# One decoder step on one core: the gate moved into the GpSimd scaling, the samples' keys loaded ahead of the cache copies, three sample products issued later

## The chip, the core and the metric

The kernel runs on one core of a Trainium2 chip. A core has five engines with instruction queues of their own: TensorE (PE, matrix products; PEld is its weight load), VectorE (DVE), ScalarE (ACT), GpSimd (POOL) and SyncE (SP), which here only issues DMAs. Each engine takes its instructions in the order in which they stand, and a waiting instruction holds up all that stand behind it on that engine. The metric is the time of one execution on the device in microseconds (us), as the median of the runs; lower is better.

## The reference

One layer of a hybrid decoder runs over a prompt of 1024 rows and over 8 samples of one row each. A projection feeds three groups of heads; what the change touches are the attention group ("NSA", 8 query heads, 2 KV heads of 64), and the samples' part of the recurrent group.

```python
def masked_softmax(s, mask):
    ...
    p = jnp.exp(s - m)
    return p / jnp.maximum(jnp.sum(p, axis=-1, keepdims=True), 1e-30)

def gate_mix(g, o_c, o_s, o_w):            # g = sigmoid of 24 projected columns, 3 per head
    return g[..., 0:1] * o_c + g[..., 1:2] * o_s + g[..., 2:3] * o_w
```

`o_c` attends to compressed blocks, `o_s` to the selected blocks (for this prompt length all the causal rows), and `o_w` to a window of 512 rows. A sample's window is `win_buf` (511 rows of its cache and one new row), and the shifted window is an output too:

```python
    kw = jnp.concatenate([win_buf, rows_w_new], axis=0)
    o_w = window_attend(q, qpos, kw[:, 0], kw[:, 1], kpos)
    return gate_mix(gates, o_c, o_s, o_w), kw[s_len:]
```

The recurrent group (RWKV-7) takes one step of its state for each sample, normalizes the result by head, and multiplies it into the sample's row.

## The kernel before

**Stages.** Phase 1 (`phase1`, up to about 515 us) projects the prompt and runs its recurrence. It also makes the gates: `do_g` turns the 24 gate columns, takes a sigmoid by way of tanh, and replaces it by its reciprocal (line 426), so that `self.gates` holds 1/gate.

Phase 2 (`phase2`, about 515 to 844 us) is the prompt's attention, with the samples' work woven in. The prompt is cut into 8 tiles of 128 rows, taken from tile 7 down to tile 0, and each tile into 4 units of two heads. For a unit, `attn_scores` does the following for each of the two branches b (0: causal, 1: window):

- PE makes the scores `p_s` in PSUM.
- DVE adds the mask, takes the row's minimum of the negated scores (`nm`) and writes `p` (line 1322; in the profile a custom instruction and a short read of the accumulator).
- ACT takes the exponential in place and sums the rows into `sm` (line 1323).
- DVE makes `fac` = 1 / (max(sm, 1e-30) / gate) in two instructions (lines 1345 and 1346).
- POOL multiplies `p` by `fac` (line 1349, one instruction for each of two heads, over 128 partitions and up to 1024 elements).

Then PE turns `p` (`p_pT<-ident,p`, `attn_turn`) by way of PSUM, ACT and DVE copy the turned blocks to `pt` in alternation (lines 1293 and 1295), and PE multiplies them with the values (`p_o<-pt,vs`, `attn_out`). DVE multiplies the result into `cat`. The compressed branch (`attn_cmp`, once a tile) makes a factor `c_r` for 8 heads in the same way (lines 1267 and 1269) and multiplies its `pcq` on DVE.

**What sets the order.** `InOrder` keeps PE's instructions in the order in which the program is written, and adds up an estimate of their time (`clock`). Four generators run beside the units: queries, tiles, samples and the samples' rests. After each piece of a unit `slot` lets those continue whose announced time has passed: a `yield 9.0` says "not before 9 us of PE's estimated time". So these numbers decide where in PE's order a sample's product stands. On the other engines the scheduler decides, by priority. DMAs stand in the order of SP's queue.

**The samples.** `sample_setup` normalizes and rotates the samples' queries and keys: a first product `p_sn` (sums of squares), later `p_sh` (the halves swapped), later `p_ts` (turned to rows). `sample_mem` and then `sample_win` each take two groups of four samples. In `sample_win`, `load` issues for each sample a copy of its cache from DRAM to DRAM (line 1800, 511 KB), the keys (`wkt`, line 1801, 256 KB), a DVE copy that puts the new key in column 0 (line 1802; it waits for the keys to land), the values (`wxv`, line 1805) and the new value's row (line 1806, which waits until the values have landed). Then PE makes `p_wS` from four samples' keys. `four_keys` takes the buffers for the keys: for each group two of a kind of their own, and two from a ring of three that `sample_mem` also uses. The load of a tile's queries (`q<-q_d`, line 1220) is in the same SP queue, and waits until POOL has split the queries (`qhl`, line 1226) that last stood in that buffer.

`sample_rwkv` takes the recurrent step on DVE, sends the result through DRAM once to bring it into rows (`rw_a<-sy_d`), normalizes it in some 20 DVE instructions (lines 2163 to 2174), and PE turns the result (`p_sy`). Then `nsa_ahead` loads `w1a` into the buffer that `p_sy` has read, and the first pages of the samples' cache.

Phase 3 (844 us to the end) makes the output projection and the samples' compressed and selected attention.

Of the kernel before, what the change touches and what calls it, by code (L numbers as in the profile page):

```python
# [15 lines left out]
OP = mybir.AluOpType  # L16
# [32 lines left out]
def bc(ap, shape):  # L49
    return ap.to_broadcast(shape)  # L50


def wait(us):
    yield us
# [60 lines left out]
class Step:  # L115
# [302 lines left out]
    def do_g(self, H, pieces, j):  # L418
        turned = self.to_tok(H, pieces, 24, 10)

        def gates():
            nc, ps = self.nc, turned()
            g = self.gates[:, H * 4:H * 4 + 4, :]
            nc.scalar.activation(g, ps[:, :, :24], AF.Tanh, scale=0.5)
            nc.vector.tensor_scalar(g, g, 0.5, 0.5, op0=OP.mult, op1=OP.add)
            nc.vector.reciprocal(g, g)
        return gates

    def phase1(self):
# [809 lines left out]
    def attn_cmp(self, i):  # L1239

        nc = self.nc
        V, A, G, PE = nc.vector, nc.scalar, nc.gpsimd, self.te
        qs = self.qs[i]
        gate = self.gates[:, i, :].rearrange("p (h b) -> p h b", b=3)
        p2 = self.pM.tile([128, 4, 2, 64], F32, name="p_sc", tag="m")
        x = 56 - 8 * i
        PE.matmul(p2[:].rearrange("p a b c -> p (a b) c"), self.cmask[:, 120:248],
                  bc(self.cmask[:, None, x:x + 64], [128, 8, 64]), start=True, stop=False)
        for j in range(4):
            for g in range(2):  # L1250
                for n, ck in enumerate((self.ckh, self.ckl)):
                    PE.matmul(p2[:, j, g], qs[:, 4 * g + j, :], ck[:, 0, g * 64:g * 64 + 64], start=False, stop=(j == 3 and g == 1 and n == 1))
            if j == 1:
                yield 0.1
        pcq = self.we.tile([128, 8, 64], F32, name="pcq", tag="pcq")
        v3 = lambda x: x.rearrange("p a b c -> p (a b) c")
        st = self.small.tile([128, 8], F32, name="c_m")
        V.tensor_reduce(st[:], v3(p2[:]), axis=AX.X, op=OP.max)
        V.tensor_scalar(st[:], st[:], -1.0e20, None, op0=OP.max)
        V.tensor_tensor(pcq[:], v3(p2[:]), bc(st[:, :, None], [128, 8, 64]), op=OP.subtract)  # L1260
        yield
        A.activation(pcq[:], pcq[:], AF.Exp)
        sm = self.small.tile([128, 8], F32, name="c_s")
        V.tensor_reduce(sm[:], pcq[:], axis=AX.X, op=OP.add)
        rc = self.small.tile([128, 8], F32, name="c_r")
        gh = lambda x: x.rearrange("p (h g) -> p g h", g=2)
        V.scalar_tensor_tensor(gh(rc[:]), gh(sm[:]), 1e-30, gate[:, :, 0].rearrange("p (g h) -> p g h", g=2),
                               op0=OP.max, op1=OP.mult)
        V.reciprocal(rc[:], rc[:])
        V.tensor_tensor(pcq[:], pcq[:], bc(rc[:, :, None], [128, 8, 64]), op=OP.mult)  # L1270
        yield 6.0 if i < 7 else 4.0
        self.pcT[i] = self.pt_copy(lambda j: pcq[:, 2 * j:2 * j + 2, :].rearrange("p a b -> p (a b)"), "c")
        yield
# [24 lines left out]
    def attn_scores(self, i, g, hp, Ps):  # L1298

        nc = self.nc  # L1300
        V, A, PE = nc.vector, nc.scalar, self.te
        n1 = 128 * (i + 1)
        w0 = max(0, 128 * (i - 4))
        split = i >= 4
        qs = self.qs[i]
        gate = self.gates[:, i, :].rearrange("p (h b) -> p h b", b=3)
        nm = self.small.tile([128, 2, 2], F32, name="nm")
        sm = self.small.tile([128, 2, 2], F32, name="sm")

        def scores(ps, q, b, c0, c1):  # L1310
            u, o, w = c0 // 512, c0 % 512, c1 - c0
            PE.matmul(ps, q, self.kh[u][:, 2 * b + g, o:o + w], start=True, stop=False)
            PE.matmul(ps, q, self.kl[u][:, 2 * b + g, o:o + w], start=False, stop=True)

        def weigh(ps, h, b, c0):
            x, w = Ps[h, b][:, :n1 - c0], n1 - c0
            if b == 1 and split:
                m = bass.AP(tensor=self.bmask.tensor, offset=self.bmask.offset, ap=[self.bmask.ap[0], [832, 2], [1, 320]])
                halves = lambda t: t.rearrange("p (a c) -> p a c", a=2)
            else:  # L1320
                m, halves = self.bmask[:, 1152 - w:1152], lambda t: t
            V.tensor_tensor_reduce(halves(x), halves(ps), m, -1.0, 3.0e38, op0=OP.add, op1=OP.min, accum_out=nm[:, h, b:b + 1])  # L1322
            A.activation(x, x, AF.Exp, scale=-1.0, bias=nm[:, h, b:b + 1], accum_out=sm[:, h, b:b + 1])  # L1323

        f = self.small.tile([128, 2, 2], F32, name="fac")
        hd = 4 * g + 2 * hp
        for b in range(2):
            c0 = w0 if b else 0
            for h in range(2):
                Ps[h, b] = self.pp.tile([128, 1024 if b == 0 else 640], F32, name="p", tag=f"p{b}")  # L1330
            if split:
                for h in range(2):
                    ps = self.pS.tile([128, 1024], F32, name="p_s", tag="s")
                    scores(ps[:, c0:512], qs[:, hd + h, :], b, c0, 512)
                    scores(ps[:, 512:n1], qs[:, hd + h, :], b, 512, n1)
                    weigh(ps[:, c0:n1], h, b, c0)
                    if h == 0:
                        yield
            else:
                ps = self.pS.tile([128, 2, 512], F32, name="p_s", tag="s")  # L1340
                for h in range(2):
                    scores(ps[:, h, :n1], qs[:, hd + h, :], b, 0, n1)
                for h in range(2):
                    weigh(ps[:, h, :n1], h, b, 0)
            V.scalar_tensor_tensor(f[:, :, b], sm[:, :, b], 1e-30, gate[:, hd:hd + 2, 1 + b], op0=OP.max, op1=OP.mult)
            V.reciprocal(f[:, :, b], f[:, :, b])  # L1346
            for h in range(2):
                x = Ps[h, b][:, :n1 - c0]
                nc.gpsimd.tensor_scalar(x, x, f[:, h, b:b + 1], None, op0=OP.mult)  # L1349
            yield  # L1350

    def attn_turn(self, i, Ps, n, m):
# [259 lines left out]
    def sample_setup(self):  # L1612

        tc, nc, I, O = self.tc, self.nc, self.I, self.O
        V, A, G, PE = nc.vector, nc.scalar, nc.gpsimd, self.te
# [14 lines left out]
        x, sq, xr = (self.we.tile([128, 8, NS], F32, name=f"s_x{k}") for k in range(3))  # L1630
# [3 lines left out]
        A.activation(x[:, 4:6], ts[:, 6:9:2, :], AF.Copy)  # L1634
        A.activation(x[:, 6:8], ts[:, 11:13, :], AF.Copy)
        A.activation(sq[:], x[:], AF.Square)
        yield 3.0
        fl = lambda t: t.rearrange("p c s -> p (c s)")
        ps = self.pM.tile([128, 512], F32, name="p_sn", tag="m")
        PE.matmul(ps[:, 0:64], sums, fl(sq[:]), start=True, stop=True)  # L1640
# [8 lines left out]
        V.tensor_tensor(o[:, 0:4], xr[:, 0:4], many(0, 4), op=OP.mult)  # L1649
        V.tensor_tensor(o[:, 4:6], xr[:, 4:6], tab[:, 1:3], op=OP.mult)  # L1650
        V.tensor_tensor(o[:, 6:8], xr[:, 6:8], many(3, 2), op=OP.mult)
        yield 9.0

        ps = self.pM.tile([128, 512], F32, name="p_sh", tag="m")
        for k in range(4):
# [128 lines left out]
    def sample_win(self):  # L1784

        nc, I, O = self.nc, self.I, self.O
        V, A, G, PE = nc.vector, nc.scalar, nc.gpsimd, self.te
# [4 lines left out]
        def load(a):  # L1792
            KT = self.four_keys("wkt", 2 + a)
            for k in range(4):
                s = 4 * a + k
                if s % 2 == 0:
                    X.append(self.slot(s // 2, [128, 2, 4, 128], F32, f"wxv{s // 2}"))
                rows = lambda t, r, ap: bass.AP(tensor=t.tensor, offset=t.offset + (s * 512 + r) * 256, ap=ap)
                with self.tc.issue_after(self.last_z.ins):
                    nc.sync.dma_start(rows(co, 0, [[8176, 16], [1, 8176]]), rows(ci, 1, [[8176, 16], [1, 8176]]))  # L1800
                nc.sync.dma_start(KT[k], I["c_wink"][s])
                V.tensor_copy(KT[k][:, 0:1], self.kwT[:, s:s + 1])
                x = X[s // 2][:, s % 2]
                part = lambda t, r, ap: bass.AP(tensor=t.tensor, offset=t.offset + (s * 512 + r) * 256 + 128, ap=ap)
                nc.sync.dma_start(x, part(ci, 0, [[1024, 128], [256, 4], [1, 128]]))
                nc.sync.dma_start(x[0:1, 0], part(co, 511, [[256, 1], [1, 128]]))
            return KT
# [20 lines left out]
        for a in range(2):  # L1828
            KT = nxt
# [7 lines left out]
            p = self.we.tile([128, 512], F32, name="w_p", tag="s_p")  # L1837
# [194 lines left out]
    def sample_rwkv(self):  # L2032
        tc, nc, I, O = self.tc, self.nc, self.I, self.O
        V, A, G, PE = nc.vector, nc.scalar, nc.gpsimd, self.te
# [11 lines left out]
        wd, a = t8("p (c s) -> p c s", 2, NS), t8("p (c s) -> p c s", 2, NS)  # L2046
# [125 lines left out]
        V.tensor_tensor(y, y, h4(lnw[:, 1]), op=OP.add)  # L2172
        V.tensor_tensor(y2, h4(vr[:, 5]), b4(bn), op=OP.mult)
        V.tensor_tensor(y, y, y2, op=OP.add)
        yield from wait(6.0)
        py = self.pM.tile([128, 2, NS], F32, name="p_sy", tag="m")
        for c in range(2):
            PE.transpose(py[:, c, :], y[:, 2 * c:2 * c + 2, :].rearrange("p h d -> p (h d)"), self.ident[:NS, :NS])
# [192 lines left out]
```

## Time and profile before

| | before |
|---|---|
| median of 3 runs | 1011.61 us (1010.33 to 1012.93) |
| the profiled execution | 1008.02 us |
| its span, first to last instruction | 1006.3 us |
| mean granted TensorE clock | 0.983 |
| busy: PE, DVE, ACT, POOL | 942.7, 680.5, 442.9, 252.6 us |
| POOL's scalings, line 1349 | 128 instructions, 208.8 us |

A row of a list of groups gives line, engine, operation, out<-in, shapes and count, then the busy time and the mean of one in ns, then the idle time of the engine just before and who ended it. A row of a timeline gives the start and the duration in us, engine, line, operation and count, and in brackets the idle time before it and who ended it. In a table of windows each engine has its busy microseconds (and number of instructions), and then follow the clock that PE was granted, the share of the DMA engines and the GB/s.

### The profile page before, as it was taken

The page shows a single profiled execution, that of the slowest core. Times are in us where ns is not written, and L with a number is a line of the kernel's source. Part 1 is how long each engine was busy: PE and PEld are TensorE (multiplying, and loading weights), DVE is VectorE, ACT ScalarE, POOL GpSimd, SP SyncE. Part 2 cuts the span into 40 slices and gives each one's busy share as a digit, 9 for nine tenths or more (in the row PEclk, how much of TensorE's full clock was granted, in tenths as well). Part 3 has the DMA queues.
Part 4 walks back from the last instruction along what each step waited for, and adds up shares of the span by engine and source line. Part 5 has one row for each costly group of instructions (what it writes and reads, how often), then busy time and mean ns, then how long its engine had stood idle before and what let it go on. Part 6 is the DMA issues. An engine that isn't in the chain of part 4 may idle for free. (4 is left out here: it accounts for less than half of the span.)

```text
span 1006.3 us, 24739 instructions
## 1 busy us (share of the span) xinstructions
PE 942.7 (94%) x9851; PEld 793.3 (79%) x9851; DVE 680.5 (68%) x2114; ACT 442.9 (44%) x989; POOL 252.6 (25%) x222
## 2 busy tenths in 40 slices
PE   7999999999999999999977989989999978999997
PEld 7988888778887877788866878868878866877864
DVE  7669489646774996634467757675879976356465
ACT  6664324323532422224345656655676644223212
POOL 2000000000000000000028766746778742112010
PEclk9999999999999999999998999999999978999999
DMA  8322213213230162354353232511200153985422
GB/s 281 106 64 69 60 45 112 67 44 90 69 107 24 36 168 66 85 151 108 107 167 126 86 111 85 156 32 40 75 19 11 37 139 116 318 282 169 149 74 76
DMA packets 133835, 103.81 MB, mean 103 GB/s; under 512 B 34577, under 2 KB 121112, under 8 KB 133592
## 3 DMA queue, kind: packets, MB, share of 16 engines
q1 hardware_dynamic: 128760, 90.53, 30.5%
q0 software_dynamic: 3200, 10.49, 3.0%
q8 instruction: 78, 1.28, 0.5%
q10 hardware_dynamic: 1760, 1.21, 0.4%
q14 instruction: 37, 0.30, 0.1%
HBM read 83.61 MB, written 22.78 MB: 106 GB/s over the span
## 5 line engine op out<-in xcount | busy, mean ns | idle before, releaser
L1349 POOL TENSOR_SCALAR p<-p,fac 128x640 f32<-128x640 f32 (+7 forms) x128 | 208.8, 1647 | 92.6 <-DVE fac L1346 33.0
L87 PE MATMUL p_pr<-h,whi 128*128 128x512 f32 (+5 forms) x928 | 230.9, 340 | 0.1
L87 PEld LDWEIGHTS p_pr<-h,whi 128*128 128x128 f32 (+1 forms) x928 | 147.3, 184 | 18.8 <-issue 2.7
L87 PE MATMUL p_pr<-h,wlo 128*128 128x512 f32 (+5 forms) x464 | 152.5, 329 | 0.0
L1323 ACT ACTIVATE p<-p,nm 128x640 f32<-128x640 f32 (+7 forms) x128 | 93.1, 728 | 63.5 <-DVE nm L1322 59.7
L999 POOL MEMSET w2d<- 128x128 f32 x1 | 0.2, 206 | 398.0 <-PE p_yy L87 398.0
L87 PEld LDWEIGHTS p_pr<-h,wlo 128*128 128x128 f32 (+1 forms) x464 | 85.1, 183 | 9.6
L284 PE MATMUL p_pr<-h,whi 128*128 128x256 f32 (+2 forms) x416 | 86.8, 304 | 0.2
L87 PE MATMUL p_pT<-ident,p 128*128 128x128 f32 x528 | 74.9, 287 | 11.5 <-POOL p L1349 5.9
L87 PEld LDWEIGHTS p_pT<-ident,p 128*128 128x128 f32 x528 | 58.9, 144 | 24.3 <-issue 9.9
L87 PE MATMUL p_o<-pt,vs 128*64 128x128 f32 x1056 | 70.6, 283 | 1.6 <-DVE sm_m L1403 1.1
L1322 DVE CUSTOM_DVE_ANT_0 p<-p_s,bmask 128x512 f32<-128x512 f32 (+7 forms) x96 | 60.1, 662 | 14.7 <-PE p_s L87 10.2
L284 PEld LDWEIGHTS p_pr<-h,whi 128*128 128x128 f32 x416 | 66.1, 188 | 3.5 <-ACT whi L273 0.6
L87 PE MATMUL p_s<-kh,qs 128*128 128x512 f32 (+3 forms) x191 | 66.3, 359 | 0.9 <-DVE nm L1322 0.9
L87 PEld LDWEIGHTS p_o<-pt,vs 128*64 128x64 f32 x1056 | 59.3, 141 | 9.7 <-issue 6.2
L274 DVE TENSOR_TENSOR wlo<-wraw,whi 128x1024 fp32r<-128x1024 f32 (+1 forms) x34 | 40.7, 1197 | 35.1 <-ACT whi L273 35.0
L284 PE MATMUL p_pr<-h,wlo 128*128 128x256 f32 (+2 forms) x208 | 62.6, 303 | 0.0
L87 PE MATMUL p_s<-kl,qs 128*128 128x512 f32 (+3 forms) x192 | 60.8, 337 | 0.0
L273 ACT ACTIVATE whi<-wraw 128x1024 fp32r<-128x1024 f32 (+1 forms) x35 | 36.3, 1038 | 49.7 <-PE p_pr L87 36.7
L1295 DVE COPY pt<-p_pT 128x512 f32<-128x512 f32 (+1 forms) x72 | 48.1, 670 | 12.6 <-PE p_pT L87 12.3
L87 PE MATMUL p_out<-woh,chi 128*128 128x512 f32 x128 | 52.8, 412 | 1.5 <-ACT woh L2191 1.4
L87 PE MATMUL p_out<-wol,chi 128*128 128x512 f32 x128 | 51.3, 401 | 1.1 <-DVE wol L2192 1.0
(535 smaller groups left out, 1951.1 us busy)
## 6 DMA issues: line engine op xcount, KB each, us to landing
wraw<-in_w_in_dram SPq DMA_DIRECT2D x34, 512.0 KB
pg<-in_c_pool_dram SPq DMA_DIRECT2D x40, 256.0 KB
pg<-in_c_pool_dram SPq DMA_DIRECT2D x48, 128.0 KB
x<-in_x_prompt_dram SPq DMA_DIRECT2D x8, 512.0 KB
z_d<-zt SPq DMA_DIRECT2D x16, 256.0 KB
cat<-z_d SPq DMA_DIRECT2D x8, 512.0 KB
wor<-in_w_out_dram SPq DMA_DIRECT2D x16, 256.0 KB
xres<-in_x_prompt_dram POOLq DMA_DIRECT2D x16, 256.0 KB, 3.7
```

What stands on the lines that cost most here:

```text
L87: self.last = getattr(self.engine, op)(*a, **k)
L273: nc.scalar.activation(hi[:, :, :n], raw[:, :, :n], AF.Copy)
L274: (low or nc.vector).tensor_tensor(lo[:, :, :n], raw[:, :, :n], hi[:, :, :n].bitcast(F32), op=OP.subtract)
L284: self.last_mm = self.pe.matmul(ps[:m, :b - a], w[:, k, :m], h[k][:, a:b], start=(k == 0 and i == 0), stop=(k == 7 and i == 2))
L999: nc.gpsimd.memset(w2d[:], 0.0)
L1295: nc.vector.tensor_copy(pt[:, :n], ps[:, :n])
L1322: V.tensor_tensor_reduce(halves(x), halves(ps), m, -1.0, 3.0e38, op0=OP.add, op1=OP.min, accum_out=nm[:, h, b:b + 1])
L1323: A.activation(x, x, AF.Exp, scale=-1.0, bias=nm[:, h, b:b + 1], accum_out=sm[:, h, b:b + 1])
L1349: nc.gpsimd.tensor_scalar(x, x, f[:, h, b:b + 1], None, op0=OP.mult)
```

## The change

The gates stay sigmoids. `attn_scores` takes only the reciprocal of `sm` on DVE, and POOL's scaling takes two factors for each row: the reciprocal and the gate. The limit of 1e-30 is left out there. `attn_cmp` now makes its factor in three DVE instructions (limit, reciprocal, multiplication with the gate). In `sample_win` the loads of four samples' keys and the DVE copies into them come before the loop that issues the cache copies and the values. Three announced times grow: 3 to 6 us before `p_sn`, 9 to 13 us before `p_sh`, and 6 to 14 us before `p_sy`.

```diff
@@ do_g
             g = self.gates[:, H * 4:H * 4 + 4, :]
             nc.scalar.activation(g, ps[:, :, :24], AF.Tanh, scale=0.5)
             nc.vector.tensor_scalar(g, g, 0.5, 0.5, op0=OP.mult, op1=OP.add)
-            nc.vector.reciprocal(g, g)
@@ attn_cmp
-        gh = lambda x: x.rearrange("p (h g) -> p g h", g=2)
-        V.scalar_tensor_tensor(gh(rc[:]), gh(sm[:]), 1e-30, gate[:, :, 0].rearrange("p (g h) -> p g h", g=2),
-                               op0=OP.max, op1=OP.mult)
+        gh = rc[:].rearrange("p (h g) -> p g h", g=2)
+        V.tensor_scalar(rc[:], sm[:], 1e-30, None, op0=OP.max)
         V.reciprocal(rc[:], rc[:])
+        V.tensor_tensor(gh, gh, gate[:, :, 0].rearrange("p (g h) -> p g h", g=2), op=OP.mult)
@@ attn_scores
-            V.scalar_tensor_tensor(f[:, :, b], sm[:, :, b], 1e-30, gate[:, hd:hd + 2, 1 + b], op0=OP.max, op1=OP.mult)
-            V.reciprocal(f[:, :, b], f[:, :, b])
+            V.reciprocal(f[:, :, b], sm[:, :, b])
             for h in range(2):
                 x = Ps[h, b][:, :n1 - c0]
-                nc.gpsimd.tensor_scalar(x, x, f[:, h, b:b + 1], None, op0=OP.mult)
+                nc.gpsimd.tensor_scalar(x, x, f[:, h, b:b + 1], gate[:, hd + h, 1 + b:2 + b], op0=OP.mult, op1=OP.mult)
@@ sample_setup
         A.activation(sq[:], x[:], AF.Square)
-        yield 3.0
+        yield 6.0
...
         V.tensor_tensor(o[:, 6:8], xr[:, 6:8], many(3, 2), op=OP.mult)
-        yield 9.0
+        yield 13.0
@@ sample_win, load
             for k in range(4):
                 s = 4 * a + k
+                nc.sync.dma_start(KT[k], I["c_wink"][s])
+                V.tensor_copy(KT[k][:, 0:1], self.kwT[:, s:s + 1])
+            for k in range(4):
+                s = 4 * a + k
                 if s % 2 == 0:
                     X.append(self.slot(s // 2, [128, 2, 4, 128], F32, f"wxv{s // 2}"))
...
                     nc.sync.dma_start(rows(co, 0, [[8176, 16], [1, 8176]]), rows(ci, 1, [[8176, 16], [1, 8176]]))
-                nc.sync.dma_start(KT[k], I["c_wink"][s])
-                V.tensor_copy(KT[k][:, 0:1], self.kwT[:, s:s + 1])
@@ sample_rwkv
         V.tensor_tensor(y, y, y2, op=OP.add)
-        yield from wait(6.0)
+        yield from wait(14.0)
```

How the change moves instructions, at three places. On PE near the end of phase 2, where `p_sy` stands; before:

```order
L87 MATMUL p_s<-kl_6306,qs 128x128
L87 MATMUL p_s<-kh_6305,qs 128x128
L87 MATMUL p_s<-kl_6306,qs 128x128
L87 MATMUL p_sy<-ident,rw_a_10231 128x8 x2
L87 MATMUL p_pTm<-ident,pmem 128x128 x4
L87 MATMUL p_o<-pt,vs_6307 64x128 x8
L87 MATMUL p_o<-pt,cvk 64x128 x2
```

and with the change:

```order
L87 MATMUL p_om<-ptm,mv 64x128 x8
L87 MATMUL p_o<-pt,vs_6305 64x128 x8
L87 MATMUL p_o<-pt,cvk 64x128 x2
L87 MATMUL p_pT<-ident,pcq 128x128 x4
L87 MATMUL p_pT<-ident,p 128x128 x4
L87 MATMUL p_sy<-ident,rw_a_10196 128x8 x2
L87 MATMUL p_sm<-mkh,qs 128x256
L87 MATMUL p_sm<-mkl,qs 128x256
```

`p_sy` moved back by 29 rows, behind the turning of the last tile's compressed branch; the rows that it passed keep their order.

On SP, the queue of the samples' window loads, from the second load of memory keys on; before:

```order
L1801 DMA wkt<-in_c_wink_dram 128x512
L1805 DMA wxv_8323<-in_cache_win_dram 128x4x128
L1800 DMA out_dram<-in_cache_win_dram 16x8176
L1806 DMA wxv_8323<-out_dram 1x128
L1801 DMA wkt<-in_c_wink_dram 128x512
L1805 DMA wxv_8420<-in_cache_win_dram 128x4x128
L1800 DMA out_dram<-in_cache_win_dram 16x8176
L1220 DMA q<-q_d 128x768
L1806 DMA wxv_8420<-out_dram 1x128
L1801 DMA wkt<-in_c_wink_dram 128x512
L1805 DMA wxv_8420<-in_cache_win_dram 128x4x128
```

and with the change:

```order
L1805 DMA wxv_8314<-in_cache_win_dram 128x4x128
L1794 DMA wkt<-in_c_wink_dram 128x512 x3
L1806 DMA wxv_8314<-out_dram 1x128
L1802 DMA out_dram<-in_cache_win_dram 16x8176
L1219 DMA q<-q_d 128x768
L1794 DMA wkt<-in_c_wink_dram 128x512
L1805 DMA wxv_8414<-in_cache_win_dram 128x4x128
L1802 DMA out_dram<-in_cache_win_dram 16x8176
```

Three of the second group's four keys now stand ahead of the queries' load, where one stood; the fourth stands right behind it, and the second group's values all stand behind it.

On DVE, the copies into the second group's keys; before, around the last two:

```order
L1346 RECIPROCAL fac<-fac 128x2
L1264 TENSOR_REDUCE c_s<-pcq 128x8
L1267 SCALAR_TENSOR_TENSOR c_r<-c_s,gates 128x2x4
L1269 RECIPROCAL c_r<-c_r 128x8
L1270 TENSOR_TENSOR pcq<-pcq,c_r 128x512
L1802 COPY wkt<-s_o 128x1 x2
L1701 TENSOR_REDUCE rs_m<-p_wS 128x1
```

and with the change, around the last one:

```order
L1705 TENSOR_SCALAR w_p<-w_p,rs_s 128x512
L1344 RECIPROCAL fac<-sm 128x2
L1380 TENSOR_TENSOR cat_8128<-cat_8128,p_o 128x128
L1294 COPY pt<-p_pT 128x512
L1795 COPY wkt<-s_o 128x1
L1398 TENSOR_REDUCE nm_m<-p_sm 128x2
L1321 ISA p,nm<-p_s,bmask 128x768
```

The last copy stands some 50 rows further ahead than before, between a copy of turned blocks and the first mask instruction of the next unit.

## The prediction

> **What bounds the kernel now.** I read the page's totals first, then windows by stage, then PE's waits in the attention stage, and last the timelines around the three places that the edits touch.
>
> ```profile
> span 1006.3 us, 24739 instructions
> PE 942.7 (94%) x9851; PEld 793.3 (79%) x9851; DVE 680.5 (68%) x2114; ACT 442.9 (44%) x989; POOL 252.6 (25%) x222
> ...
> 524.00:811.00 287.00, 264.42 (x2592) 224.35 (x2590) 220.33 (x658) 179.70 (x445) 207.52 (x125) 0.98 0.25 76
> 811.00:836.00 25.00, 17.97 (x168) 15.46 (x168) 16.22 (x75) 10.54 (x41) 9.60 (x16) 0.80 0.45 110
> ...
> 760.00:800.00 40.00, 38.37 (x414) 33.72 (x412) 38.77 (x127) 26.82 (x81) 30.38 (x25) 1.00 0.08 23
> ```
>
> PE is busy for 94% of the span, so an edit pays only where it removes PE's idle time or the low clock behind it. In 524 to 811 PE has 264.42 of 287 us. The one loose stretch is 811 to 836: 17.97 of 25, at a clock of 0.80. POOL, which gets more to do, looks idle by its 25%, but has 207.52 of 287 in this stage and 30.38 of 40 at 760 to 800. DVE is full there (38.77 of 40). PE's waits name who came last:
>
> ```profile
> PE p_sy L87 <- issue: 6.7, 1, 6.7
> PE p_pT L87 <- POOL p L1349: 5.9, 5, 2.5
> PE p_wS L87 <- DVE wkt L1802: 3.9, 1, 3.9
> ```
>
> (total us, times, longest). The first and the third are what the moved products and loads aim at; the second lies behind the scaling that grows.
>
> **The change: `p_sy` (term e).**
>
> ```profile
> 810.17 0.28 PE L87 MATMUL p_s<-kl,qs 128*128 128x128 f32 x1
> 817.11 0.34 PE L87 MATMUL p_sy<-ident,rw_a 8*128 8x8 f32 x2 [6.66 <-issue]
> 820.76 1.97 PE L87 MATMUL p_pT<-ident,p 128*128 128x128 f32 x8
> 822.81 0.37 PE L87 MATMUL p_s<-kh,qs 128*128 128x128 f32 x1
> 823.89 1.09 PE L87 MATMUL p_o<-pt,vs 128*64 128x128 f32 x16
> ...
> 816.60 0.41 DVE L2174 TENSOR_TENSOR rw_a<-rw_a 8x256 f32<-8x256 f32 x1
> ```
>
> PE stands still from 810.45 to 817.11; the profile calls it issue, but DVE's last normalizing instruction ends at 817.01, so it is the wait for `rw_a`. Behind it the same eight turnings take 1.97 us where at 801 they took 1.10:
>
> ```profile
> 801.52 1.10 PE L87 MATMUL p_pT<-ident,p 128*128 128x128 f32 x8 [0.30 <-issue]
> ```
>
> So PE does the 5.70 us from 817.11 to 822.81 at about 1.10/1.97 of its rate: 3.2 us of work, a tail of 2.5. Idle and tail are 9.2. `p_sy` now stands 29 rows later, behind work that DVE has to feed; DVE is not quicker by the move, and a copy of turned blocks that PE needs sits behind the same chain of normalizing instructions. I therefore leave 1.7 to a wait that appears there: **+7.5** (5.5, if a new wait keeps 3.7 of it; 9.2, if none). [...]
>
> Late next could be the load of `w1a` into the buffer that `p_sy` reads:
>
> ```profile
> 817.48 4.65 SPq L961 DMA_DIRECT2D w1a<-in_cmp_w_dram  x4
> 844.51 3.81 PE L87 MATMUL p_hid<-pg,w1a 128*128 128x128 f32 x32
> 824.00:826.00 2.00, 2.00 (x28) 1.83 (x29) 1.38 (x11) 1.65 (x8) 0.48 (x1) 1.00 0.08 15
> ```
>
> The DMAs are quiet from 824 (share 0.08), so it lands some 7 us after its issue and is needed at 844.51: 20 us of cover. `p_sy` moves by 4 to 5 us at most. Nothing.
>
> **`p_wS` and the keys (terms c and b).**
>
> ```profile
> 658.31 0.21 DVE L1802 COPY wkt<-s_o 128x1 f32<-128x1 f32 x2
> 658.51 1.52 PE L87 MATMUL p_wS<-wkt,qb 128*32 128x512 f32 x4 [3.86 <-DVE wkt L1802]
> 662.97 1.53 PE L87 MATMUL p_pT<-ident,p 128*128 128x128 f32 x12
> 656.51 4.38 POOL L1349 TENSOR_SCALAR p<-p,fac 128x768 f32<-128x768 f32 x2 [4.25 <-ACT pcq L1262]
> ```
>
> The last two copies of the second group's keys end at 658.52 and PE has waited 3.86 for them. With the keys loaded earlier that wait goes. But the next turnings need POOL's two scalings, which end at 660.9 whatever PE does; there PE would then wait. I take **+2.0** (0, if POOL's end holds all of it; 5, wait plus a clock tail as above).
>
> The price is on DVE. Its copy waits for the key's load, and the eighth now stands ahead of the mask instructions of a unit, its load right behind that of the queries:
>
> ```profile
> 635.23 0.36 SPq L1220 DMA_DIRECT2D q<-q_d  x1
> 635.87 0.69 DVE L1295 COPY pt<-p_pT 128x512 f32<-128x512 f32 x1 [0.25 <-PE p_pT L87]
> 593.11 0.89 SPq L1801 DMA_DIRECT2D wkt<-in_c_wink_dram  x2
> 597.58 0.15 DVE L1802 COPY wkt<-s_o 128x1 f32<-128x1 f32 x1 [4.45 <-DMA wkt<-in_c_wink_dram]
> 600.18 1.95 PE L87 MATMUL p_pT<-ident,p 128*128 128x128 f32 x12 [2.02 <-DVE cat L1429]
> ```
>
> The queries' load waits for POOL until 635.23. Going by the first key (issued 593.11, copied 597.58) the eighth lands near 640, while DVE reaches its copy near 636.5: a stall of about 3.4, with the unit's masks, exponentials and scalings queued behind it. At 597 a stall of 4.45 cost PE 2.02, and its turnings (1.95 for 12) ran slow as well, some 1.6 more by the ratio above. I take **−2.5** (0, if the scores already made cover it; −4.5, all of DVE's 4.45).
>
> **The start of the stage and `p_sh` (term a).**
>
> ```profile
> 523.48 0.16 DVE L1345 SCALAR_TENSOR_TENSOR fac<-sm,gates 128x2 f32<-128x2 f32 x1 [1.23 <-ACT p L1323]
> 524.37 0.16 DVE L1346 RECIPROCAL fac<-fac 128x2 f32<-128x2 f32 x1
> 524.71 9.40 POOL L1349 TENSOR_SCALAR p<-p,fac 128x1024 f32<-128x1024 f32 x4 [0.16 <-DVE fac L1346]
> 530.44 3.65 PE L87 MATMUL p_pT<-ident,p 128*128 128x128 f32 x15 [2.50 <-POOL p L1349]
> 547.23 0.29 PE L87 MATMUL p_sh<-s_x,ident 128*32 128x48 f32 x8 [1.68 <-DVE pt L1295]
> ```
>
> `fac` is made in two instructions 0.89 us apart, with a mask between; with one, POOL starts up to 0.9 earlier, and PE waits 2.50 for POOL at 530.44. `p_sh` waits 1.68 for a copy that frees a buffer; the product behind it takes a buffer of the same kind and inherits most of that. **+1.0** (−0.5, if it is later than what follows; 2.6, 0.9 and 1.68). `p_sn` has no wait to lose.
>
> **DVE's relief (term d).**
>
> ```profile
> L1345 DVE SCALAR_TENSOR_TENSOR fac<-sm,gates 128x2 f32<-128x2 f32 x64 | 12.1, 189 | 13.8 <-ACT p L1323 12.8
> 740.00:817.00 77.00, 66.70 (x671) 58.15 (x669) 71.09 (x240) 49.59 (x143) 59.65 (x48) 0.97 0.14 42
> ```
>
> 64 instructions, 12.1 us in all, go from DVE; the compressed branch adds 8 short ones (1.5 at 189 ns), and the gates' two reciprocals lie in phase 1, where no wait for them shows. Only where DVE is the fuller engine does this count: 740 to 817 (71.09 of 77), a quarter of the units, so 3 us of DVE, of which PE, nearly full itself, returns a part: **+1.0** (0 to 3).
>
> **POOL's second factor (term f).** No instruction of before scales by two factors.
>
> ```profile
> L1349 POOL TENSOR_SCALAR p<-p,fac 128x1024 f32<-128x1024 f32 x8 | 22.7, 2846 | 3.7 <-issue 2.4 <-DVE fac L1346 1.3
> L1349 POOL TENSOR_SCALAR p<-p,fac 128x128 f32<-128x128 f32 x16 | 9.6, 617 | 15.6 <-PE p_pT L87 10.5 <-DVE cat L1382 2.3 <-ACT pcq L1262 1.5
> L1349 POOL TENSOR_SCALAR p<-p,fac 128x640 f32<-128x640 f32 (+7 forms) x128 | 208.8, 1647 | 92.6 <-DVE fac L1346 33.0
> L629 POOL MEMSET scanm<- 128x512 f32 x1 | 0.5, 524 | 0.0
> L999 POOL MEMSET w2d<- 128x128 f32 x1 | 0.2, 206 | 398.0 <-PE p_yy L87 398.0
> L1226 POOL TENSOR_TENSOR qhl<-q,qhl 128x256 fp32r<-128x256 f32 x15 | 11.3, 751 | 68.7 <-ACT qhl L1225 68.0 <-DMA out_dram<-nr_y 0.7
> ```
>
> One factor costs (2846 − 617)/(1024 − 128) = 2.49 ns per element and 300 ns fixed. Writing alone costs (524 − 206)/384 = 0.83, so reading and one multiplication are at most 1.66. The bounds of the second multiplication: 0, if it hides in the loop (a gain is excluded: the same elements move), and another 1.66. All 128 instructions have (208.8 − 128 × 0.30)/2.49 ns = 68,000 elements, so that is up to 113 us. I take **0**, by the nearest row: the subtraction for `qhl` reads two inputs, does one operation and writes, for (751 − 300)/256 = 1.76. A scaling reads one input less and yet costs 2.49, so its loop is bound neither by moving data nor by one operation, and may hold room for a second already. [...]
>
> **Sum:** +1.0 − 2.5 + 2.0 + 1.0 + 7.5 + 0 = 9.0. The profiled execution took 1008.0 (1.7 around its span), so 999.0; it lies 3.6 under the median 1011.6 of the runs shown, so 1002.6 there: **1002.5 us**.
>
> **Rivals.** *POOL becomes the bound.* Its place is the units of 524 to 811, its price the second multiplication. At 760 to 800 some 22.9 of POOL's 30.38 grow with the size (25 fixed parts of 0.30 off); they meet PE's 38.37 when an element is 35% dearer, by 0.87 ns. From there every unit waits for POOL. At the upper bound of 1.66 some 107 of the 113 us fall into the stage: 314 where 287 are there, 27 over, of which the gains behind the stage (e) give back a part: about 1033. At 0.87 the stage is still whole, but with POOL, DVE and PE all full in the window the gains go: 1011. I put this rival in the middle, at 1022. For it: an operation in a loop costs something, and PE already waits 5.9 us for POOL; against: the subtraction's row.
>
> *The waits only move.* DVE's chain that made `p_sy` late holds up the next copy of turned blocks instead, so e is only the 3.2 us of work that comes forward; the eighth key costs its full 4.5, POOL's end keeps c at 0, and a is 0. With d, −0.3: 1011.9, no change. For it: DVE is full at 760 to 817 either way. Against: `p_o` at 823.89 needs its copy well after 817.
>
> *Everything pays:* a 2, b 0, c 4, d 2, e 9 make 17, 994.6. It ends on the forecast's side.
>
> **How the numbers follow.** The forecast, the case where everything pays with it, has 0.68 (its own range 995 to 1008), POOL as the bound 0.20, the moved waits 0.12. Three us, 0.3%, are about what a measurement can tell from no change. The forecast gives 0.63 to faster and 0.05 to same; the moved waits 0.02, 0.08 and 0.02; POOL 0.02 to same and 0.18 to slower: 0.65, 0.15, 0.20. The range of 995 to 1016 leaves out about 0.06 below, where everything pays and more, and 0.14 above, POOL's dearer part.
>
> **What would show it.** POOL's scaling of 128x1024 in the groups: 2846 is term f as taken, over 3500 the first rival, and then PE's wait for `p` by POOL grows from 5.9 to tens of us. PE's wait list without `p_sy`, and a clock near 0.9 in 811 to 836, is e; a new wait of 3 us or more for `pt` at 811 to 820 is the second rival. A DVE wait of 3 to 4.5 for a DMA of `wkt` near 636 is b; PE's wait on `wkt` near 658 gone, and one for POOL in its stead, is c. The prediction is wrong at its root if the stage from 524 to 844 gets no shorter although these waits are gone.

## The result and the profile after

The changed kernel takes 986.37 us (median; 984.51 to 988.05) where the kernel before takes 1010.97: 0.9755 of it (95% interval 0.973 to 0.978), 24.6 us less. In a second measurement, beside the last experiments, it took 985.99 against 1011.2, 0.9765 (0.9741 to 0.9789). The time lies 16 us under the forecast of 1002.5 and 9 under the range; the direction was right, the size was not. The traces show 20.0 of the 24.6 us: the profiled execution is the slowest of the changed kernel's four (988.05) and a quick one of the kernel before (1008.02).

Where it went shows in two windows of the same length of work: from the first scores of the prompt's attention to the first product of phase 3. First the kernel before, then the changed one, each in its own window (columns as in the tables of windows above):

```profile
515.77:844.51 328.74, 297.04 (x2868) 251.56 (x2869) 245.60 (x764) 196.25 (x496) 218.14 (x143) 0.95 0.28 82
```

```profile
517.17:823.60 306.43, 287.43 (x2869) 245.49 (x2869) 239.51 (x708) 195.81 (x496) 119.32 (x143) 0.99 0.30 89
```

The stage is 22.3 us shorter, of 20.0 by which the span shrank (1006.3 to 986.3); what lies ahead of it came 1.4 later, and phase 3 is no quicker. PE has the same matmuls in it. Its idle time went from 31.7 to 19.0, which is 12.7; the other 9.6 are the same matmuls in less busy time, with the clock at 0.99 instead of 0.95. The column to look at is POOL's: 218.14 to 119.32. The groups of the changed kernel say why:

```profile
L1347 POOL TENSOR_SCALAR p<-p,fac,gates 128x640 f32<-128x640 f32 (+7 forms) x128 | 109.4, 866 | 162.9 <-DVE fac L1344 104.2
...
L1347 POOL TENSOR_SCALAR p<-p,fac,gates 128x1024 f32<-128x1024 f32 x8 | 9.9, 1253 | 3.0 <-DVE fac L1344 2.3 <-DVE c_m L1258 0.7
L1347 POOL TENSOR_SCALAR p<-p,fac,gates 128x128 f32<-128x128 f32 x16 | 7.5, 480 | 10.4 <-DVE fac L1344 10.4
```

The scaling by two factors takes 1253 ns at 128x1024; by one it took 2846. That is (1253 − 480)/896 = 0.86 ns per element in place of 2.49. What the prediction treated as an added cost halved POOL's work. PE's waits in the stage:

```profile
PE p_pT L87 <- DVE cat L1280: 2.7, 1, 2.7
PE p_pT L87 <- DVE pcq L1269: 2.4, 1, 2.4
...
PE p_pT L87 <- POOL p L1347: 0.5, 1, 0.5
```

The waits for `rw_a` (6.7) and `wkt` (3.9) are gone, and that for POOL fell from 5.9 to 0.5. What is left is short, and the longest two are for DVE.

### The profile page after: what moved, and what is told of

It is laid out like the page before. It is cut to its first block, busy times and chain, and to the rows that moved or that the text cites. A ratio compares the mean times of both kernels' runs of the same rounds, so it can differ in the third digit from the quotient of the medians.

```text
span 986.3 us, 24664 instructions
## 1 busy us (share of the span) xinstructions
PE 934.6 (95%) x9851; PEld 788.9 (80%) x9851; DVE 673.2 (68%) x2056; ACT 442.4 (45%) x989; POOL 153.3 (16%) x222
## 4 chain that ended last, share of the span: by engine, by line
PE 67%; DVE 15%; ACT 7%; DMA 5%; issue 3%; SPq 2%; POOL 0%; ACTq 0%; DVEq 0%; POOLq 0%
PE p_pr L87 20%; PE p_pr L284 8%; PE p_out L87 5%; PE p_pT L87 5%; PE p_s L87 5%; PE p_o L87 4%; ACT p L1322 3%; PE p_hid L87 2%; DMA x<-in_x_prompt_dram 2%; PE p_iy L87 2%; PE p_z L87 1%; DVE p L1321 1%; PE p_it L87 1%; DVE pt L1294 1%; PE p_sc L87 1%
## 5 line engine op out<-in xcount | busy, mean ns | idle before, releaser
L1347 POOL TENSOR_SCALAR p<-p,fac,gates 128x640 f32<-128x640 f32 (+7 forms) x128 | 109.4, 866 | 162.9 <-DVE fac L1344 104.2
L87 PE MATMUL p_pT<-ident,p 128*128 128x128 f32 x528 | 72.6, 281 | 8.6 <-DVE cat L1280 2.7
L87 PE MATMUL p_o<-pt,vs 128*64 128x128 f32 x1056 | 67.9, 277 | 0.4 <-DVE shid L1009 0.4
L87 PEld LDWEIGHTS p_o<-pt,vs 128*64 128x64 f32 x1056 | 57.0, 137 | 7.5 <-issue 4.4
```

Source lines behind the costliest of these rows:

```text
L87: self.last = getattr(self.engine, op)(*a, **k)
L1347: nc.gpsimd.tensor_scalar(x, x, f[:, h, b:b + 1], gate[:, hd + h, 1 + b:2 + b], op0=OP.mult, op1=OP.mult)
```

## The experiments

Two theories went into the runs. **Rate:** the quick scalings carry more than half of the 24.6 us, since POOL stood in the chain of every unit. **Waits:** the moved product and loads, and the clock behind them, carry it, and quick scalings return only the 5.9 us in which PE waited for POOL.

### The rate alone

On the kernel before, a second operation that changes no value; no instruction moves on any engine.

```diff
-                nc.gpsimd.tensor_scalar(x, x, f[:, h, b:b + 1], None, op0=OP.mult)
+                nc.gpsimd.tensor_scalar(x, x, f[:, h, b:b + 1], 1.0, op0=OP.mult, op1=OP.mult)
```

> The kernel before, with one thing changed: the GpSimd scaling multiplies by fac and then by the constant 1.0 instead of by fac alone. No instruction moves on any engine. If the second operand makes the scaling quick whatever it is, the 128x1024 scaling takes about 1250 ns instead of 2846. Theory 'rate' (scalings at half the time carry more than half of the 24.6 us): 993 to 998 us against 1011. Theory 'waits' (the moved products and loads and the clock behind them carry it; quicker scalings return only the 5.9 us in which PE waited for POOL): 1004 to 1007. If only a second row factor, not a constant, makes it quick: 2846 ns and 1011.

Measured: 1000.28 us against 1010.19, 0.9901 (0.9876 to 0.9926): 9.9 us. Groups and PE's waits of this run:

```profile
L1349 POOL TENSOR_SCALAR p<-p,fac 128x1024 f32<-128x1024 f32 x8 | 8.9, 1124 | 10.5 <-DVE fac L1346 4.7 <-DMA y_rw<-y_d 4.0 <-DMA mv<-out_dram 1.7
L1349 POOL TENSOR_SCALAR p<-p,fac 128x128 f32<-128x128 f32 x16 | 5.8, 372 | 20.2 <-PE p_pT L87 11.0 <-PE p_sm L87 3.1 <-ACT ptm L1414 2.5
```

```profile
PE p_sy L87 <- issue: 6.7, 1, 6.7
PE p_wS L87 <- DVE wkt L1802: 4.3, 1, 4.3
...
515.77:836.70 320.93, 295.45 (x2868) 251.43 (x2869) 246.84 (x768) 195.92 (x499) 103.77 (x143) 0.95 0.28 85
```

A constant does it as well: 0.84 ns per element. The wait for POOL has left the list, and the waits for `rw_a` and `wkt` stand as they stood. The last row is the stage in this run, 7.8 us shorter than before: 6.2 less idle, about the 5.9 of the waits for POOL, and 1.6 less busy. The median time lies between the two theories' ranges: more than the 5.9, less than half of the whole. Neither holds by itself.

The same from the other side: the changed kernel with one factor, which leaves out the gate of the two branches.

```diff
-                nc.gpsimd.tensor_scalar(x, x, f[:, h, b:b + 1], gate[:, hd + h, 1 + b:2 + b], op0=OP.mult, op1=OP.mult)
+                nc.gpsimd.tensor_scalar(x, x, f[:, h, b:b + 1], None, op0=OP.mult)
```

> The changed kernel, but the scaling takes one factor only (the gate of these two branches is left out of the computation); all other instructions stand as in the changed kernel. The scaling should go back to about 2850 ns at 128x1024. Theory 'rate': the time rises by 13 to 18 us from 986.4, to 999 to 1004, and PE's waits for p by POOL come back. Theory 'waits': it rises by about 6, to 991 to 994.

Measured: 995.64 us, 0.9852 (0.982 to 0.9884) of the kernel before; 9.3 over the changed kernel. The slow price is back, and so are waits for POOL, though only 2.9 us of them:

```profile
L1347 POOL TENSOR_SCALAR p<-p,fac 128x1024 f32<-128x1024 f32 x8 | 22.7, 2844 | 2.9 <-DVE c_m L1258 1.5 <-DVE fac L1344 1.4
...
PE p_pT L87 <- POOL p L1347: 2.9, 4, 2.1
```

Added or taken away, the rate is worth 9 to 10 us, and both times the time lies between the two theories' ranges. Here the waits that bear POOL's name are a third of it. The traces tell where most of the rest lies: from the first scores to `p_k`, the first turning of the memory keys, the changed kernel takes 31.2 us (517.17 to 548.35), and with one factor 37.0 (518.64 to 555.61). So 5.8 of the 7.1 us between the two profiled executions fall in the units at the start of the stage, the ones with the longest scalings. On the kernel before the same stretch shrinks by 2.7 only, from 37.0 to 34.3, and the rest of the gain lies further on.

### What makes a scaling slow

Two price lists on the kernel before, in which the four pairs of branch and head each take another form (in the second, extra instructions behind the scaling that change no value).

```diff
+                if (b, h) == (0, 0):
+                    nc.gpsimd.tensor_scalar(x, x, s1, None, op0=OP.mult)
+                elif (b, h) == (0, 1):
+                    nc.gpsimd.tensor_scalar(x, x, s1, 1.0, op0=OP.mult, op1=OP.mult)
+                elif (b, h) == (1, 0):
+                    nc.gpsimd.tensor_scalar(x, x, 1.0, s1, op0=OP.mult, op1=OP.mult)
+                else:
+                    nc.gpsimd.tensor_scalar(x, x, s1, 0.0, op0=OP.mult, op1=OP.add)
```

> A price list of the scaling on the kernel before: branch 0, first head: fac alone; branch 0, second head: fac, then times 1.0; branch 1, first head: 1.0, then times fac; branch 1, second head: fac, then plus 0.0. The computed values stay the same. If any second operation makes it quick, the three latter take about 880 ns at 128x640 and the first 1886. If it is the kind of operand (a row factor in the first place) that is slow, the third alone differs.

```profile
L1357 POOL TENSOR_SCALAR p<-p,fac 128x640 f32<-128x640 f32 x16 | 13.2, 826 | 0.0
L1355 POOL TENSOR_SCALAR p<-p,fac 128x640 f32<-128x640 f32 x16 | 12.8, 798 | 38.6 <-DVE cat L1390 11.0 <-ACT pt L1293 10.8 <-DVE fac L1346 6.3
...
L1351 POOL TENSOR_SCALAR p<-p,fac 128x640 f32<-128x640 f32 x4 | 7.5, 1885 | 14.1 <-DVE fac L1346 8.3 <-ACT pt L1293 5.8
...
L1353 POOL TENSOR_SCALAR p<-p,fac 128x640 f32<-128x640 f32 x4 | 3.2, 800 | 0.0
```

Lines 1351, 1353, 1355 and 1357 are the four forms in the order of the diff. Each second operation tried here makes it quick, in either place, multiplication (800 and 798 ns) or addition (826), where one operation takes 1885; a single run of the whole kernel took 1002.58 us.

```diff
+                if (b, h) == (0, 1):
+                    nc.gpsimd.tensor_scalar(x, x, 1.0, None, op0=OP.mult)
+                elif (b, h) == (1, 0):
+                    nc.gpsimd.tensor_scalar(x, x, 1.0, 1.0, op0=OP.mult, op1=OP.mult)
+                elif (b, h) == (1, 1):
+                    nc.gpsimd.tensor_copy(x, x)
```

> A second price list on the kernel before: branch 0, first head: fac alone as before; all other scalings by fac and 1.0, and behind them, as an extra instruction that changes no value, for branch 0, second head: times the constant 1.0 alone; branch 1, first head: times 1.0 and times 1.0; branch 1, second head: a copy onto itself. If one operation alone is slow whatever its operand, times 1.0 alone takes about 1886 ns at 128x640 and the pair 800; if only a single row factor is slow, times 1.0 alone takes 800 or less. The copy gives the price of moving the data: at most 800 if the quick form is bound by moving. The time itself says nothing here (work is added).

```profile
L1357 POOL TENSOR_SCALAR p<-p 128x640 f32<-128x640 f32 x16 | 11.8, 739 | 0.0
L1359 POOL COPY p<-p 128x640 f32<-128x640 f32 x16 | 11.5, 716 | 0.0
...
L1355 POOL TENSOR_SCALAR p<-p 128x640 f32<-128x640 f32 x4 | 7.4, 1846 | 0.3
```

One constant alone is slow too (1846), two constants take 739, and a copy, which does no arithmetic, 716. So it isn't the row factor: one multiplication alone takes a slow form, by a row factor (1886 in this run) or by a constant, and the form with two takes about what the copy takes. Why the form with one is slow, no run here shows.

### The moved product alone

```diff
-        yield from wait(6.0)
+        yield from wait(14.0)
```

> The kernel before with p_sy announced 14 instead of 6 us later, and nothing else. The prediction's term e: -7.5 (5.5 to 9.2), so 1003.5 us (1002 to 1005.5). Theory 'waits': -9 or a little more, 1001 to 1002. Theory 'rate': the work that comes forward meets the slow scalings of the last tiles, so -4 to -7, 1004 to 1007.

Measured on the kernel before: 1000.7 us, 0.9912 (0.9883 to 0.9941), 9.5 us (6 to 12). Timeline and PE's waits:

```profile
813.70 0.63 PE L87 MATMUL p_pT<-ident,p 128*128 128x128 f32 x4 [0.54 <-DVE rq_t L136]
819.77 0.66 PE L87 MATMUL p_om<-ptm,mv 128*64 128x128 f32 x8 [0.68 <-DVE pt L1295]
820.14 0.39 DVE L2174 TENSOR_TENSOR rw_a<-rw_a 8x256 f32<-8x256 f32 x1
822.48 0.28 PE L87 MATMUL p_sy<-ident,rw_a 8*128 8x8 f32 x2
...
PE p_pT L87 <- POOL p L1349: 6.3, 6, 2.4
```

The normalization ends 3.5 us later than before, and PE finds it ready all the same. Two small new waits for DVE, 0.54 and 0.68, are what the chain leaves. The wait for POOL grew by only 0.4: the work that came forward did not meet the slow scalings, which the rate theory expected; the time is at the waits theory's edge. The 9.5 are just over the upper bound of the prediction's term, 9.2, and their interval holds the whole of its range.

Undone in the changed kernel (14.0 back to 6.0):

> The changed kernel with p_sy announced 6 us later as before. The prediction's term e taken away from the changed kernel: 7.5 up from 986.4, 994 (992 to 996). Theory 'rate': with quick scalings PE runs further ahead of the samples' normalization, so that the wait grows and it costs as much or more, 994 to 998. Theory 'waits' (most of the gain is in this place): 996 to 1000.

Measured: 992.65 us, 0.9827 (0.9805 to 0.9849), 6.3 over the changed kernel.

```profile
804.84 0.35 PE L87 MATMUL p_sy<-ident,rw_a 8*128 8x8 f32 x2 [2.79 <-ACT p L1322]
...
797.75:829.00 31.25, 26.38 (x273) 22.69 (x271) 21.36 (x99) 16.28 (x54) 10.10 (x21) 0.89 0.33 82
```

and the same stretch of the changed kernel, from the same matmul on:

```profile
797.00:823.60 26.60, 24.23 (x273) 20.49 (x271) 21.00 (x99) 16.18 (x54) 10.56 (x21) 1.00 0.38 96
```

The wait is 2.79 here, not 6.66; of the 4.65 us by which the stretch is longer, 2.15 are the same 273 matmuls in more busy time, with the clock at 0.89 instead of 1.00, and 2.5 are idle. The time is at the low end of the prediction's term, and under what both theories expected.

### The gate part alone

The kernel before with the gates left as sigmoids, one reciprocal and POOL's two factors, as in the diff of the change; the rest as before.

> The kernel before with the whole gate part: gates left as sigmoids, one reciprocal on DVE for fac, two factors on POOL. Against the scaling by fac and 1.0 this adds only what DVE loses (64 instructions of 189 ns) and POOL's earlier start. The prediction's terms d and part of a, 1 to 2 us: 1 to 2 us quicker than the kernel before with fac and 1.0. Theory 'rate': 991 to 997 us. Theory 'waits': 1002 to 1006.

Measured: 996.54 us, 0.9863 (0.9843 to 0.9883). Against the kernel before with 1.0 as second factor that is 3.7 more (the two intervals just overlap), for which DVE's relief, POOL's earlier start and the order that follows are left. It lies in the rate theory's range, and 2 to 3 us under the 998 to 999 that the prediction's terms give. PE's waits:

```profile
PE p_wS L87 <- DVE wkt L1800: 4.5, 1, 4.5
...
PE p_sy L87 <- ACT p L1322: 2.8, 1, 2.8
```

The wait at `p_sy` shrank from 6.7 to 2.8 though `p_sy` was not moved. It is the largest change among PE's waits between the two runs, but it isn't all DVE's doing: DVE ends the normalization 1.2 us earlier than with 1.0 as second factor (811.62 against 812.78), and PE comes to `p_sy` 2.8 later (808.94 against 806.14). That DVE is earlier because it has 64 instructions fewer is argued, not shown; their order changed too. A second place is the start of the stage: from the first scores to `p_k` it takes 31.7 us (519.54 to 551.26) where it took 34.3 (516.86 to 551.19). Elsewhere this trace loses what it gains there: its execution is the slowest of the four (999.56), as long as the other one (999.97). So how the 3.7 us of the medians divide is not shown.

### The keys

The kernel before with the keys loaded ahead, and the changed kernel with the keys as before (the lines of the change in `load`, done or undone).

> The kernel before with the four keys of a group loaded ahead of the cache copies and the values, and nothing else. The prediction: +2.0 for p_wS less 2.5 for a new DVE wait on the eighth key near 636, about 1011 (1008 to 1014). Theory 'waits': p_wS's 3.9 and its slow clock go, 1005 to 1008. Theory 'rate': POOL's end of the two 128x768 scalings holds the next turnings, 1010 to 1012.

> The changed kernel with the keys loaded one by one between the cache copies as before. The prediction's terms b and c nearly cancel: 986 to 988. Theory 'rate': with quick scalings nothing hides the wait for the keys at p_wS any more (PE comes there earlier while the loads do not), so 4 to 8 up, 990 to 994. Theory 'waits': 3.9 and the slow clock behind it, 990 to 992.

Done alone: 1010.53 us, 0.9997 (0.9977 to 1.0017), nothing. Undone in the changed kernel: 991.04, 0.9824 (0.9801 to 0.9846), 4.7 up. The same edit is worth nothing beside slow scalings and about 5 us beside quick ones. The timelines tell why; keys done alone:

```profile
632.96 0.33 SPq L1220 DMA_DIRECT2D q<-q_d  x1
633.73 0.33 SPq L1796 DMA_DIRECT2D wkt<-in_c_wink_dram  x1
637.06 0.15 DVE L1797 COPY wkt<-s_o 128x1 f32<-128x1 f32 x1 [2.64 <-DMA wkt<-in_c_wink_dram]
641.69 0.66 PE L87 MATMUL p_pT<-ident,p 128*128 128x128 f32 x4 [2.11 <-DVE fac L1346]
653.24 1.07 PE L87 MATMUL p_wS<-wkt,qb 128*32 128x512 f32 x8
656.07 1.09 PE L87 MATMUL p_pT<-ident,p 128*128 128x128 f32 x8
656.20 4.38 POOL L1349 TENSOR_SCALAR p<-p,fac 128x768 f32<-128x768 f32 x2 [4.33 <-ACT w_p L1703]
660.21 0.66 PE L87 MATMUL p_pT<-ident,p 128*128 128x128 f32 x4 [3.05 <-DVE cat L1281]
672.53 0.63 PE L87 MATMUL p_spT<-ident,w_p 128*128 128x128 f32 x4
```

the changed kernel:

```profile
625.39 0.33 SPq L1219 DMA_DIRECT2D q<-q_d  x1
625.84 0.36 SPq L1794 DMA_DIRECT2D wkt<-in_c_wink_dram  x1
629.13 0.16 DVE L1795 COPY wkt<-s_o 128x1 f32<-128x1 f32 x1
646.13 1.07 PE L87 MATMUL p_wS<-wkt,qb 128*32 128x512 f32 x8
652.74 1.05 PE L87 MATMUL p_pT<-ident,p 128*128 128x128 f32 x4 [2.69 <-DVE cat L1280]
665.04 0.63 PE L87 MATMUL p_spT<-ident,w_p 128*128 128x128 f32 x4
```

and the changed kernel with the keys as before:

```profile
649.58 1.05 PE L87 MATMUL p_wS<-wkt,qb 128*32 128x512 f32 x4
655.08 1.99 PE L87 MATMUL p_wS<-wkt,qb 128*32 128x512 f32 x4 [4.45 <-DVE wkt L1800]
672.02 0.63 PE L87 MATMUL p_spT<-ident,w_p 128*128 128x128 f32 x4
```

With slow scalings the queries' load waits for POOL until 632.96, the eighth key behind it lands at 637, DVE stands 2.64 and PE 2.11. With quick ones the load goes out at 625.39 and the copy at 629.13 waits for nothing. In both a wait of about 3 us for DVE stands where `p_wS` had waited for the keys: part of that wait only changed its name. It is not the wait for POOL that the prediction expected: with slow scalings eight of the twelve next turnings run at 656.07, ahead of POOL's two scalings (656.20 to 660.58), and the other four start before these end, so that none of them needs them, and PE's waits for POOL stay at 5.9.

The same PE work can be timed in each run. From `p_wS` of the second group to `p_spT`, the turning of its weights, the kernel before takes 21.0 us (653.60 to 674.60) and the keys alone 19.3: 1.7 gained. From `p_wS` of the first group to its `p_spT`, across the eighth key, they take 13.1 (629.43 to 642.56) and 14.9 (627.30 to 642.18): 1.75 lost, so nothing is left. In the changed kernel the second stretch takes 18.9, with the keys as before 22.4, which is 3.5 gained, and the first takes 13.15 (621.96 to 635.11): nothing lost.

### The setup's two products

The changed kernel with 3 and 9 us again ahead of `p_sn` and `p_sh`.

> The changed kernel with p_sn and p_sh announced 3 and 9 us later as before. What stands on record for it is at most the wait of 1.68 at p_sh with its neighbours (part of term a). Theory 'rate': the quick scalings have made this place as loose as the others, 986 to 988. Theory 'waits': 2 to 3 up from the changed kernel, 988 to 990.

> The changed kernel once more, beside the runs of this call: 986 us (984.5 to 988), as first measured.

Measured: 989.68 us, 0.9782 (0.9755 to 0.9809), beside 985.99, 0.9765 (0.9741 to 0.9789), of the changed kernel in the same measurement. The medians differ by 3.7, the two ratios by only 1.7 us, and the intervals overlap: whether this part is worth anything is not settled. The wait of 1.7 at `p_sh` is among PE's waits neither here nor in the run of the rate alone, so with quick scalings it is gone without the move.

### A try for more

POOL is now busy for 119 us of 306 in the stage. The changed kernel with the scaling of the memory branch's weights on POOL in the quick form, and then with the product for `pcq` there too:

```diff
-            V.tensor_tensor(pm[:], pm[:], bc(sm[:, :, None], [128, 2, 256]), op=OP.mult)
+            for h in range(2):
+                G.tensor_scalar(pm[:, h, :], pm[:, h, :], sm[:, h:h + 1], 1.0, op0=OP.mult, op1=OP.mult)
```

> The changed kernel with the scaling of the memory branch's weights (pmem, on DVE 16 of 760 ns, 12.2 us) on GpSimd, as 32 scalings of 128x256 by the reciprocal and 1.0 (about 520 ns each by the first run, 17 us in all). GpSimd has about 187 us free in the stage. Theory 'rate' (PE waits for chains, of which GpSimd no longer is the slow link, and DVE is now): 2 to 4 quicker than the changed kernel, 982 to 984. Theory 'waits': PE is bound by its own work, no change, 985 to 988.

> As the last, and the product of pcq with its factor (on DVE 8 of 767 ns) on GpSimd too, as a product of two tensors, at 1.76 ns per element and 300 fixed about 1.2 us each. Theory 'rate': DVE loses 6 us more but the chain through pcq, for which PE waits 2.4 at the start of the stage, gets 0.5 longer; 980 to 985. Theory 'waits': 985 to 990.

Measured: 985.68 us, 0.9749 (0.9727 to 0.977), and 984.39, 0.9729 (0.9704 to 0.9754), beside 985.99. The first gains nothing, as the waits theory had it, though its 32 scalings take only 493 ns each; the second may gain 1.6, which the intervals don't tell from none. So taking these two products off DVE did not shorten the kernel by a measurable amount.

## Why the prediction was wrong, and where it was right

**Term f, POOL's second factor, is the step that failed.** The prediction bounded the second multiplication from 0 to 1.66 ns per element and wrote "a gain is excluded: the same elements move". It took the form for the sum of its operations. The runs showed another form: 0.86 ns per element in place of 2.49, and a copy at nearly the same price (716 ns at 128x640, two constants 739). The gain it excluded is 9.9 us alone and 9.3 in the changed kernel. The rows to see it were there: the subtraction with two inputs cost 1.76 by the prediction's own working, a memset 0.83, so that 2.49 for one input and one multiplication was too much for either, and the prediction read from it only that there was "room for a second already".

**Term d, DVE's relief, was mis-sized:** with its share of a some 1 to 2 us, where the gate part beyond the rate brought about 3.7. The prediction spread 3 us of DVE's time over the units. In the trace the gain stands at two places, the start of the stage (2.6) and the wait at `p_sy`, which the prediction had costed by itself; DVE's and POOL's shares in it are not told apart.

**Term e, `p_sy`, held:** 7.5 forecast, 9.5 measured alone (6 to 12), 6.3 in the changed kernel, where the wait without the move is 2.79 and no longer 6.66. Of the 1.7 kept back for a new wait, 0.54 and 0.68 show. `w1a` cost nothing, as argued:

```profile
812.48 4.20 SPq L960 DMA_DIRECT2D w1a<-in_cmp_w_dram  x4
823.56 1.69 PE L87 MATMUL p_hid<-pg,w1a 128*128 128x128 f32 x13
```

the load is issued behind `p_sy` and PE comes to it without a wait.

**Terms b and c** had the right size for the kernel before, −0.5 together and nothing measured (−1.7 to 2.3 by the interval). In b the mechanism was right too, down to the eighth key's stall (3.4 forecast, 2.64 on DVE; PE 2.02 by the nearest row, 2.11 measured). In c the size, 2.0 against 1.7 in the trace, was luck: the prediction let POOL's two 128x768 scalings hold the next turnings, but these don't need them, and what took back part of the gain is the wait for DVE. For the whole change both were wrong: +4.7 in place of −0.5. In the traces the edit is worth 3.5 beside scalings of two factors and nothing beside those of one. About 1.75 of this is b, whose cause, the queries' buffer that POOL frees late, goes with the slow scaling and so follows from f; the other half is c, worth 3.5 where it was 1.7.

**Term a** is not settled. POOL's earlier start can't be told apart from DVE's relief in the runs. The wait of 1.68 at `p_sh` is gone as soon as the scalings are quick, and what moving `p_sh` and `p_sn` is worth lies within the noise.

The steps from the kernel before to the changed one, as measured: rate 9.9, the rest of the gate part 3.7, keys and setup together 3.9 (from 996.54 to 992.65), `p_sy` 6.3. Each is measured from the one before it, so that they add up to 23.8 by construction; the 0.8 to 24.6 lie between two medians of the kernel before. Against the sum of 9.0, f brought 9.9 where 0 was put, a to d together 7.6 where 1.5 was put, and e 6.3 where 7.5 was put. Undone singly, the keys are worth 4.7 and the setup perhaps 3.7, more than the 3.9 of both; how they share it the intervals don't settle. Of the first rival, POOL as the bound, the opposite happened; the moved waits have their place only at the keys.

## What to carry to other kernels

Compare the price per element of an instruction with that of its neighbours that move as much or more: a row that is dear for what it does may be on a slow form (here 2.49 ns with one input and one operation, against 1.76 with two inputs). Adding an operand made it quicker here (1886 ns to 810 at 128x640, by a constant), so a bound on an operation that the trace doesn't show must reach below nothing. Here an engine that was busy for 72% of a stage also held a buffer that a load waited for, and its price was more than the waits that bear its name (9.3 us against 2.9 in the changed kernel with one factor). And an edit that does nothing alone (the keys) can pay once another has removed what hid it, so parts are best measured both ways, done alone and undone from the whole.

## What the runs showed of the hardware

On GpSimd a `tensor_scalar` with one operation took 1846 to 1886 ns at 128x640, by a row factor or a constant, and with two operations, at least one of them by a constant, 739 to 826; a copy 716. Two row factors cost some 100 ns more per instruction than a row factor and a constant (480 against 372 at 128x128, 1253 against 1124 at 128x1024).

The quick form isn't equally quick everywhere: in the changed kernel 128x384 took 1052 ns on the mean, more than 128x512 with 799. The long ones lie in the last tiles:

```profile
752.70 3.03 POOL L1347 TENSOR_SCALAR p<-p,fac,gates 128x384 f32<-128x384 f32 x4 [4.26 <-DVE sm_m L1401]
760.85 4.42 POOL L1347 TENSOR_SCALAR p<-p,fac,gates 128x384 f32<-128x384 f32 x4 [5.12 <-DVE fac L1344]
...
760.00:800.00 40.00, 36.74 (x381) 32.44 (x379) 38.86 (x121) 27.04 (x81) 24.05 (x28) 1.00 0.24 71
```

Four take 3.03 us at 752 and 4.42 at 761, where DVE is full (38.86 of 40). With a row factor and 1.0 the step is there too (823 at 128x384, 709 at 128x512), so it isn't the second row factor. With one factor the mean was 1422, under the 1582 at 128x512, but over the some 1250 that 2.49 ns per element and 300 ns give. Whether DVE's load is the cause was not tried.
